# Attention on one Trainium2 core: where the softmax sums divide, the probabilities or two blocks' outputs

## The chip, the cores and the metric

The kernel runs on one core of one Trainium2 chip. The metric is the device time of one execution in microseconds (us). Three executions of the kernel before took 1732.94, 1730.12 and 1730.2 us, a median of 1730.2. The engines are called as in the profile: PE (matrix products; PEld is its weight load), DVE (vector), ACT (activation functions), POOL, and SP, which only issues DMAs; SPq, PEldq and the like are the engines' sequencers.

## What is computed

Two layers of a hybrid backbone over 512 latent tokens and 256 context tokens, width 1024. The change touches layer 0, windowed attention with a learned sink per head, 16 query heads and 4 key/value heads:

```python
def block(b):
    ...
    s_ctx = jnp.einsum('bqkgd,bnkd->bkgqn', qb, k_c, preferred_element_type=jnp.float32) * scale
    s_loc = jnp.einsum('bqkgd,bnkd->bkgqn', qb, kb, preferred_element_type=jnp.float32) * scale
    s_loc = jnp.where(valid, s_loc, NEG_INF)
    sink_col = jnp.broadcast_to(sink_g, s_ctx.shape[:-1] + (1,))
    p = jax.nn.softmax(jnp.concatenate([s_ctx, s_loc, sink_col], axis=-1), axis=-1).astype(vb.dtype)
    return (jnp.einsum('bkgqn,bnkd->bqkgd', p[..., :L], v_c)
            + jnp.einsum('bkgqn,bnkd->bqkgd', p[..., L:L + band], vb))
```

The output projection `o_x @ w_o` follows, and the same attention for the context queries over the context keys alone. Layer 1 (retention) and both feed-forward parts are untouched.

## The kernel before, in words

**Tiling.** Attention goes over four groups `g` of four query heads that share a key/value head, and in each group over six blocks of 128 queries: four latent ones, `(0, b)`, and two context ones, `(1, b)`. A block has 512, 640 or 256 keys. The order of the blocks is latent then context in groups 0 and 1, `mixed` in group 2, `late` in group 3 (L832 to L840). After blocks 1 and 3 of groups 0 to 2 the next heads' queries are made by `make_q` (L559), whose long projections on PE (L147 to L149) are the work that fills PE between the blocks' short products.

**One block.** `score` (L685) runs per head: PE multiplies queries by keys into one of three PSUM banks (L710), DVE adds the mask and takes the running extreme (L711), and per pair of heads ACT takes the exponential with the row sum (`lnexp`, shown at L101), DVE the reciprocals of the two sums (L721). Then the probabilities are divided: the second head of the pair on ACT (L725), the first on DVE (L727). `turn` (L731) transposes the four heads' probabilities per 128 keys on PE (L736) and copies them out of PSUM, in turn on ACT and on DVE (L738). `output` (L743) multiplies them by the values on PE (L750): `O` has a head's 64 features on a half of the partitions (heads 0 and 1 of the group on the lower half, 2 and 3 on the upper), and the queries along the row. In groups 0 to 2 DVE copies `O` to `o_raw`, one tile of 512 columns for a pair of blocks (L765). `splits_o` (L776) cuts `o_raw` later, during groups 2 and 3, into the high and low parts that the output projection multiplies; `parts_o` (L835) is the order of these pieces and `PARTS_AT` how many go behind each block.

**What sets the order.** The instructions are written block by block; a scheduler orders each engine's instructions by its own estimate, within the dependencies. `after(x, others)` adds an order to it: `x` stands behind `others`, with no wait on a semaphore of its own. Each engine works its list in order, and so does SP with its DMAs: in this part the next queries' halves (L605), weights (L122), and towards the end the residual streams (L181, L174). Tiles come from rings: `sq` has two buffers, shared by the squares of `make_q` (written by ACT at L585, read by PE at L617) and by later users; `res` has twelve, `stat` four, `pr` (probabilities) nine, `tt` (transposed) eight.

Of the kernel before, what the change touches and what calls it, by code (L numbers as in the profile page):

```python
# [8 lines left out]
F32 = mybir.dt.float32  # L9
# [5 lines left out]
P = 128  # L15
D = 1024
KT = D // P
SX = 512
# [3 lines left out]
NKV = 4  # L22
# [27 lines left out]
def dit_kernel(ctx, tc, xT, cT, crow, small, consts, masks, tabs0, tabs1, jtab, adaQ, adaN, adaT, wst, out):  # L50
    nc = tc.nc
# [10 lines left out]
    def T(pool, cols, tag, bufs, dt=F32):  # L62
        return pool.tile([P, cols], dt, tag=tag, bufs=bufs, name=tag)
# [27 lines left out]
    def after(ins, others):  # L91
        for o in others:
            tc.add_manual_dep(ins.ins, o.ins.name, order, reason="table set turn")
# [69 lines left out]
    def split(t, hi, lo, behind=()):  # L163
        after(nc.scalar.copy(hi, t), behind)  # L164
        return nc.vector.tensor_tensor(lo, t, hi, op=sub)  # L165
# [19 lines left out]
    def t_sq(n):  # L185
        return T(rp, 512, "sq", 2)[:, :n]
# [186 lines left out]
    raw = []  # L373
# [294 lines left out]
    psA2 = At.enter_context(tc.tile_pool(name="psA2", bufs=1, reuse_waits="tile", space=PSUM))  # L668
    pS = lambda: T(psA2, 512, "S2", 3)

    run_dep = mybir.DependencyInfo(mybir.DependencyClass.Sync, mybir.DependencyReason.DATA)
    o_raw = {}
    o_t = [[None] * KT, [None] * KT]

    class Block:
# [9 lines left out]
        def score(self, i):  # L685
            g, s, b, n = self.g, self.s, self.b, len(self.keys) * P
            hd, nl = 4 * g + i, len(self.lk) * P
            if i % 2 == 0:
                self.st = T(ap, 16, "stat", 4)
            st, c = self.st, 2 * (b + 4 * s)  # L690
            qt = q[hd, s][:, b * P:(b + 1) * P]
            pt = T(ap, 656, "pr", PRB)[:, :n + 1]
            top = stats[hd][:, 1, c + hd % 2:c + hd % 2 + 1]
            nc.gpsimd.tensor_copy(pt[:, n:n + 1], top)
            lo, x0 = st[:, i % 2:i % 2 + 1], self.lk[0] * P if nl else 0

            if nl == 384:
                runs = [(nl, SC, 5 * P, [(0, SC, kc)]), (0, nl, 2 * P, [(0, nl, kx)])]
            elif nl == 0:
                runs = [(0, SC, 5 * P, [(0, SC, kc)])]  # L700
            elif b == 0:
                runs = [(0, n, 3 * P, [(0, nl, kx), (nl, SC, kc)])]
            else:
                runs = [(0, n, 0, [(0, SC, kc), (SC, nl, kx)])]
            for c0, w, m0, parts in runs:
                bank = pS()[:, :w]
                for p0, pw, kk in parts:
                    for r in range(2):
                        keys = kk[g][r] if kk is kc else kk[g][r][:, x0:x0 + pw]
                        nc.tensor.matmul(bank[:, p0:p0 + pw], qt, keys, start=r == 0, stop=r == 1)  # L710
                nc.vector.tensor_tensor_reduce(pt[:, c0:c0 + w], bank, mask[:, m0:m0 + w], 1.0, top, add, ALU.min, lo)  # L711
                top = lo
            self.pr.append(pt)
            if i % 2 == 0:
                return
            y = stats[hd][:, 0, c:c + 2]
            nc.vector.scalar_tensor_tensor(st[:, 2:4], st[:, 0:2], -1.0, y, mult, mult)  # L717
            for e in range(2):
                pt = self.pr[i - 1 + e]
                lnexp(pt, pt, AF.Exp, scale=y[:, e:e + 1], bias=st[:, 2 + e:3 + e], accum_out=st[:, 4 + e:5 + e])  # L720
            nc.vector.reciprocal(st[:, 6:8], st[:, 4:6])  # L721
            for e in range(2):
                pt = self.pr[i - 1 + e]
                if e:
                    nc.scalar.activation(pt[:, :n], pt[:, :n], AF.Identity, scale=st[:, 6 + e:7 + e])  # L725
                else:
                    nc.vector.tensor_scalar(pt[:, :n], pt[:, :n], st[:, 6 + e:7 + e], None, op0=mult)  # L727
            if i == 3:
                self.tt = []
# [13 lines left out]
        def output(self):  # L743
            g, s, b = self.g, self.s, self.b
            O = pO()[:, :256]
            for ki, (t, tt) in enumerate(zip(self.keys, self.tt)):
                vg = vt[t][:, g * HD:(g + 1) * HD]
                f, l = ki == 0, ki == len(self.keys) - 1
                for e in range(2):
                    ins = nc.tensor.matmul(O[64 * e:64 * e + 64, :], vg, tt[:, 256 * e:256 * e + 256], start=f, stop=l)  # L750
                    if f:
                        tc.add_manual_dep(ins.ins, self.last.ins.name, run_dep, reason="value products in one run")
            if g == NKV - 1:
                if b == 0:
                    for e in range(2):
                        o_t[s][2 * g + e] = h_tiles(s)
                for e in range(2):
                    hi, lo = o_t[s][2 * g + e]
                    cs = slice(b * P, b * P + P)
                    split(O[:, e * P:e * P + P], hi[:, cs], lo[:, cs])  # L760
                return
            if b % 2 == 0:
                o_raw[g, s, b // 2] = T(rp, 512, "res", 12)
            dst = o_raw[g, s, b // 2].rearrange("p (e b q) -> p e b q", e=2, b=2)[:, :, b % 2, :]
            nc.vector.tensor_copy(dst, O.rearrange("p (e q) -> p e q", e=2))  # L765

    def attend(g, s, b):
        blk = Block(g, s, b)
        for i in range(4):
            blk.score(i)  # L770
        for ki in range(len(blk.keys)):
            blk.turn(ki)
        blk.output()
        return blk.copy

    def splits_o(g, s, bp):  # L776

# [47 lines left out]
    def context_out(d, w):  # L825
# [6 lines left out]
    latent, context = [(0, b) for b in range(4)], [(1, b) for b in range(2)]  # L832
    mixed = [latent[0], latent[1], context[0], latent[2], latent[3], context[1]]
    late = [context[0], latent[0], context[1], latent[1], latent[2], latent[3]]
    parts_o = [p for sb in ((0, 0, 0), (0, 1, 0), (1, 1, 0), (2, 1, 0), (0, 0, 1), (1, 0, 0), (1, 0, 1),  # L835
                            (2, 0, 0), (2, 0, 1)) for p in splits_o(*sb)]
    PARTS_AT = {(2, 4): 2, (2, 5): 3, (3, 0): 3, (3, 1): 2, (3, 2): 2, (3, 3): 2, (3, 4): 2, (3, 5): 2}
    for g in range(NKV):
        final = g == NKV - 1
        for i, (s, b) in enumerate((latent + context, latent + context, mixed, late)[g]):  # L840
            copy = attend(g, s, b)
            if not final and i in (1, 3):
                for piece in make_q(2 * g + 2 + i // 3):
                    piece()
            if (g, i) >= SPLIT_AT:
                first = len(parts_o) == 18
                for _ in range(PARTS_AT[g, i]):
                    parts_o.pop(0)([copy])
                if first:
                    wo0 = wpos[0]  # L850
                    cres = load_stream(1)
            for d in {3: early[:1], 4: early[1:3], 5: early[3:]}.get(i, ()) if final else ():
                wpos[0] = wo0 + d
                wo_w[d] = next_w(ap, 0)
                context_out(d, wo_w[d])
# [1102 lines left out]
```

## Time and profile before

| what | us |
|---|---|
| median of three executions | 1730.2 |
| the profiled execution | 1731.61 |
| its span | 1729.8 |
| attention (first scores to last output product) | from 99 to 314 of the span |
| PE busy, whole span | 1700.0 (98%) |
| DVE busy, whole span | 1361.1 (79%) |
| ACT busy, whole span | 870.4 (50%) |

A busy PE is not a PE at its full rate: its products are pipelined, a product of 256 columns is shown with 0.28 us and follows the one before after 0.12. So the chain of waits, which follows the end back through what released each step, says more on the bound than the busy share. All durations in the prediction are of the profiled execution.

### The profile page before, as it was taken

How to read it: one execution, taken by the hardware profiler on the slowest of the kernel's cores; microseconds unless marked ns; L12 is line 12 of the kernel's file. 1: busy time of each engine (PE TensorE's matmuls, PEld its weight loads, DVE VectorE, ACT ScalarE, POOL GpSimd, SP SyncE). 2: the span in 40 equal slices, each digit the busy share in tenths (PEclk: the TensorE clock that was granted, in tenths of full speed). 3: DMA queues.
4: the chain of work that ended last, by engine and by line, in shares of the span. 5: the costliest groups of instructions: out<-in, count | busy, mean ns of one | idle time of the engine just before them, and what ended most of it. 6: DMA issues, size and time to landing. Idle time of an engine off the chain costs nothing.

```text
span 1729.8 us, 27790 instructions
## 1 busy us (share of the span) xinstructions
PE 1700.0 (98%) x10876; PEld 1515.2 (88%) x10876; DVE 1361.1 (79%) x2436; ACT 870.4 (50%) x1552; POOL 50.4 (3%) x168
## 2 busy tenths in 40 slices
PE   7999999999999999999999999999999999999999
PEld 5788877899999999999988788898897899999988
DVE  6698889798778788787889858858758798877774
ACT  5587779565434334342556534524525565445442
POOL 0000000000000000000000000000000000000000
PEclk9999999999999999999999999999999999999999
DMA  9612221643244434453423524524423223333322
GB/s 356 232 30 57 62 62 56 209 133 123 74 150 121 156 110 149 122 155 102 156 99 88 182 76 134 161 83 125 157 89 108 91 81 106 115 109 111 98 86 86
DMA packets 62803, 207.48 MB, mean 120 GB/s; under 512 B 7248, under 2 KB 8912, under 8 KB 62416
## 3 DMA queue, kind: packets, MB, share of 16 engines
q1 hardware_dynamic: 55184, 178.97, 32.5%
q0 software_dynamic: 7200, 26.22, 5.1%
q8 instruction: 85, 1.39, 0.3%
q10 hardware_dynamic: 288, 0.52, 0.1%
q14 instruction: 46, 0.38, 0.1%
HBM read 199.65 MB, written 2.10 MB: 117 GB/s over the span
## 4 chain that ended last, share of the span: by engine, by line
PE 79%; DVE 12%; DMA 5%; ACT 2%; issue 2%; SPq 0%; DVEq 0%; ACTq 0%
PE Y L897 15%; PE Z L897 8%; PE pj L147 7%; PE pj L149 7%; PE pj L148 7%; PE X L897 4%; DMA wraw<-in_wst_dram 4%; PE Z L1292 4%; DVE wlo L165 3%; PE pT L736 2%; PE pO L750 2%; PE S L710 2%; PE X L149 1%; PE X L147 1%; PE X L148 1%
## 5 line engine op out<-in xcount | busy, mean ns | idle before, releaser
L164 ACT CAST whi<-wraw 128x1024 fp32r<-128x1024 f32 x258 | 270.0, 1051 | 335.9 <-PE Z L149 80.1
L165 DVE TENSOR_TENSOR wlo<-wraw,whi 128x1024 fp32r<-128x1024 f32 x258 | 314.2, 1221 | 64.8 <-ACT whi L164 62.9
L897 PE MATMUL Y<-aq,whi 128*128 128x384 f32 x640 | 173.7, 335 | 0.0
L897 PEld LDWEIGHTS Y<-aq,whi 128*128 128x128 f32 x640 | 116.6, 188 | 1.1 <-ACT hn L1053 1.1
L256 DVE SCALAR_TENSOR_TENSOR res<-pj,mod,res 128x512 f32<-128x512 f32 (+1 forms) x112 | 81.0, 728 | 39.4 <-PE pj L149 39.2
L273 DVE CUSTOM_DVE_ANT_0 y<-adaw,crow,small_sb 128x1024 bf16<-128x1024 f32 x64 | 81.9, 1280 | 32.2 <-DMA adaw<-in_adaT_dram 32.0
L897 PE MATMUL Y<-aq,wlo 128*128 128x384 f32 x320 | 107.0, 334 | 0.0
L1292 PE MATMUL Z<-whi,sA 128*128 128x512 f32 x256 | 81.5, 393 | 1.3 <-ACT gate L1479 1.2
L101 ACT ACTIVATE pr<-pr,stat,qs 128x513 f32<-128x513 f32 (+2 forms) x96 | 74.2, 775 | 9.1 <-DVE stat L717 8.8
L147 PE MATMUL pj<-ax,whi 128*128 128x512 f32 x176 | 69.1, 393 | 0.4 <-DVE res L256 0.4
L149 PE MATMUL pj<-ax,whi 128*128 128x512 f32 x176 | 68.7, 390 | 0.0
L148 PE MATMUL pj<-ax,wlo 128*128 128x512 f32 x176 | 68.6, 390 | 0.0
L147 PE MATMUL pj<-act,whi 128*128 128x512 f32 x168 | 65.6, 390 | 0.0
L148 PE MATMUL pj<-act,wlo 128*128 128x512 f32 x168 | 65.5, 390 | 0.0
L149 PE MATMUL pj<-act,whi 128*128 128x512 f32 x168 | 65.5, 391 | 0.0
L897 PEld LDWEIGHTS Y<-aq,wlo 128*128 128x128 f32 x320 | 60.1, 188 | 0.0
L711 DVE CUSTOM_DVE_ANT_0 pr<-S,mask,qs 128x256 f32<-128x256 f32 (+1 forms) x96 | 53.1, 566 | 7.9 <-PE S L710 5.4
L1292 PEld LDWEIGHTS Z<-whi,sA 128*128 128x128 f32 x256 | 48.0, 188 | 12.6 <-ACT gate L1479 2.1
L897 PE MATMUL Y<-sA,whi 128*128 128x256 f32 x304 | 58.1, 277 | 0.1
L897 PE MATMUL Y<-hx,whi 128*128 128x256 f32 x304 | 56.3, 277 | 0.0
L736 PE MATMUL pT<-const_sb,pr 128*128 128x128 f32 x352 | 54.1, 280 | 1.2 <-ACT tt L738 0.9
L736 PEld LDWEIGHTS pT<-const_sb,pr 128*128 128x128 f32 x352 | 40.2, 142 | 12.0 <-issue 4.0
(581 smaller groups left out, 5085.4 us busy)
## 6 DMA issues: line engine op xcount, KB each, us to landing
wraw<-in_wst_dram SPq DMA_DIRECT2D x224, 512.0 KB, 3.7
adaw<-in_adaT_dram POOLq DMA_DIRECT2D x48, 512.0 KB, 3.9
wx<-in_wst_dram SPq DMA_DIRECT2D x30, 512.0 KB, 4.3
adan<-in_adaQ_dram SPq DMA_DIRECT2D x16, 512.0 KB, 8.7
adan<-in_adaN_dram SPq DMA_DIRECT2D x12, 512.0 KB, 8.1
adaw<-in_adaT_dram SPq DMA_DIRECT2D x8, 512.0 KB, 3.9
res<-in_xT_dram SPq DMA_DIRECT2D x14, 256.0 KB, 2.8
aq<-in_adaN_dram SPq DMA_DIRECT2D x12, 256.0 KB, 5.7
```

Source lines behind the costliest of these rows:

```text
L101: ins = nc.scalar.activation(*args, **kw)
L147: nc.tensor.matmul(o, whi, xhi, start=first, stop=False)
L148: nc.tensor.matmul(o, wlo, xhi, start=False, stop=False)
L149: return nc.tensor.matmul(o, whi, xlo, start=False, stop=last)
L164: after(nc.scalar.copy(hi, t), behind)
L165: return nc.vector.tensor_tensor(lo, t, hi, op=sub)
L256: return nc.vector.scalar_tensor_tensor(res[d], o, mods[l, s][:, part, d:d + 1], res[d], mult, add)
L273: res.append(nc.vector.tensor_tensor_reduce(junk, w, cr[:, s * 1024:(s + 1) * 1024], 1.0, sm_t[:, C_ADAB + l * 48 + j:C_ADAB + l * 48 + j ...
L711: nc.vector.tensor_tensor_reduce(pt[:, c0:c0 + w], bank, mask[:, m0:m0 + w], 1.0, top, add, ALU.min, lo)
L736: nc.tensor.transpose(tp[:, a * P:(a + 1) * P], self.pr[(0, 2, 1, 3)[a]][:, ki * P:(ki + 1) * P], ident)
L897: nc.tensor.matmul(o, p, r, start=first and k + i == 0, stop=k == 3 and i == 2, skip_group_check=not first)
L1292: ins = nc.tensor.matmul(os[t], p, r, start=first and k + i == 0, stop=k == 3 and i == 2, skip_group_check=by_k or not first)
```

## The change

In groups 0 to 2 the probabilities are no longer divided. The two reciprocals of each pair of heads are written by a DMA to a tile in DRAM, as rows over the queries. Two blocks after a pair of blocks is complete, two DMAs read the pair's rows back, each spread over 64 partitions, and one DVE instruction multiplies the `o_raw` tile of both blocks by them. Group 3 divides as before. The ring `stat` grows from 4 to 12 buffers, and the pieces of `(2, 1, 0)` move two places back in `parts_o`.

```diff
@@ -668,6 +668,8 @@
+    rows = At.enter_context(tc.tile_pool(name="rows", bufs=1, reuse_waits="tile", space=bass.MemoryType.DRAM))
+    factor_rows, row_end, o_end = {}, [None], [None]
@@ -686,7 +688,7 @@
             if i % 2 == 0:
-                self.st = T(ap, 16, "stat", 4)
+                self.st = T(ap, 16, "stat", 12)
@@ -719,6 +721,14 @@
             nc.vector.reciprocal(st[:, 6:8], st[:, 4:6])
+            if g < NKV - 1:
+                if i == 1 and b % 2 == 0:
+                    factor_rows[g, s, b // 2] = rows.tile([2, 2, 2, P], F32, tag="row", bufs=9, name="row")
+                row = factor_rows[g, s, b // 2][:, i // 2, b % 2, :]
+                row_end[0] = nc.sync.dma_start(row.rearrange("e q -> q e"), st[:, 6:8])
+                if i == 3:
+                    self.tt = []
+                return
             for e in range(2):
@@ -757,12 +767,12 @@
-                    split(O[:, e * P:e * P + P], hi[:, cs], lo[:, cs])
+                    o_end[0] = split(O[:, e * P:e * P + P], hi[:, cs], lo[:, cs])
                 return
...
-            nc.vector.tensor_copy(dst, O.rearrange("p (e q) -> p e q", e=2))
+            o_end[0] = nc.vector.tensor_copy(dst, O.rearrange("p (e q) -> p e q", e=2))
@@ -772,6 +782,13 @@
+    def scale_o(g, s, bp):
+        raw, factor = o_raw[g, s, bp], t_sq(SX)
+        row = factor_rows[g, s, bp].rearrange("e j b q -> e (j b q)")
+        for e in range(2):
+            after(nc.sync.dma_start(factor[64 * e:64 * e + 64, :], row[e:e + 1, :].broadcast_to([64, 512])), row_end)
+        after(nc.vector.tensor_tensor(raw, raw, factor, op=mult), o_end)
@@ -832,13 +849,18 @@
-    parts_o = [p for sb in ((0, 0, 0), (0, 1, 0), (1, 1, 0), (2, 1, 0), (0, 0, 1), (1, 0, 0), (1, 0, 1),
+    parts_o = [p for sb in ((0, 0, 0), (0, 1, 0), (1, 1, 0), (0, 0, 1), (1, 0, 0), (2, 1, 0), (1, 0, 1),
                             (2, 0, 0), (2, 0, 1)) for p in splits_o(*sb)]
+    unscaled = []
     for g in range(NKV):
...
             copy = attend(g, s, b)
+            while unscaled and unscaled[0][0] + 2 <= 6 * g + i:
+                scale_o(*unscaled.pop(0)[1])
+            if not final and b % 2:
+                unscaled.append((6 * g + i, (g, s, b // 2)))
```

Lines of the changed kernel are later by 2 to 22: L711 becomes L713, L721 L723, L727 L737, L736 L746, L738 L748, L750 L760, L765 L775. New are L728 (the write of the rows), L790 (the two reads) and L791 (the multiplication). There are 36 writes, 18 reads and 9 multiplications.

The scheduler sets many instructions elsewhere. Three places follow; `ISA` in these lists is L711's (now L713's) instruction, in two parts.

First DVE in group 0, where the first block's second pair has its reciprocals and the second block's scores come in. Before:

```order
L721 RECIPROCAL stat<-stat 128x2
L717 SCALAR_TENSOR_TENSOR stat<-stat,qs 128x2
L711 ISA pr,stat<-S_1441,mask,stat 128x384
L711 ISA stat 128x1
L727 TENSOR_SCALAR pr<-pr,stat 128x512
L711 ISA pr,stat<-S_1447,mask,qs 128x256
L711 ISA stat 128x1
L589 STREAM_SHUFFLE y_1544<-hn 128x512
L738 COPY tt<-pT 128x512
L711 ISA pr,stat<-S_1451,mask,stat 128x384
L711 ISA stat 128x1
L590 TENSOR_TENSOR hn<-hn,rope_175 128x512
```

Now:

```order
L723 RECIPROCAL stat<-stat 128x2
L713 ISA pr,stat<-S_1437,mask,qs 128x256
L713 ISA stat 128x1
L748 COPY tt<-pT 128x512
L719 SCALAR_TENSOR_TENSOR stat<-stat,qs 128x2
L713 ISA pr,stat<-S_1441,mask,stat 128x384
L713 ISA stat 128x1
L713 ISA pr,stat<-S_1447,mask,qs 128x256
L713 ISA stat 128x1
L748 COPY tt<-pT 128x512
L713 ISA pr,stat<-S_1451,mask,stat 128x384
L713 ISA stat 128x1
```

The division L727 is gone, and the two copies of transposed probabilities stand two to three places earlier among the scores.

Second SP in group 0, from block 2 to the context blocks (`q<-y` and `q<-hn` are the next queries' high and low halves, `y_1841` those that `make_q` makes behind block 3; `sq<-row` are the two reads for the first pair of blocks). Before:

```order
L122 DMA wraw<-in_wst_dram 128x1024 x2
L605 DMA q<-y_1841 64x512
L605 DMA q<-hn 64x512
L605 DMA q<-y_1841 64x512
L605 DMA q<-hn 64x512
L605 DMA q<-y_1879 64x256 x2
L605 DMA q<-hn 64x256 x2
```

Now:

```order
L728 DMA row<-stat 128x2x1 x2
L122 DMA wraw<-in_wst_dram 128x1024
L728 DMA row<-stat 128x2x1 x2
L790 DMA sq<-row 64x512 x2
L605 DMA q<-y_1841 64x512 x2
L605 DMA q<-hn 64x512 x2
L605 DMA q<-y_1879 64x256 x2
L728 DMA row<-stat 128x2x1
L605 DMA q<-hn 64x256 x2
```

The weights' load and the queries' halves stand behind writes that need a reciprocal, and the halves behind the two reads as well.

Third DVE at the end of the fourth block of group 2 (latent block 2 in the `mixed` order), where the last `make_q` runs out. Before:

```order
L592 TENSOR_TENSOR hn<-hn,y_3203 128x512
L738 COPY tt<-pT 128x512
L711 ISA pr,stat<-S_3266,mask,qs 128x512
L711 ISA stat 128x1
L609 TENSOR_TENSOR q<-hn,q 64x512
L165 TENSOR_TENSOR wlo<-wraw,whi 128x1024
L765 COPY res<-pO 128x2x128
L199 SCALAR_TENSOR_TENSOR qs<-pj,qs 128x12
L610 TENSOR_TENSOR q<-hn,q 64x512
L609 TENSOR_TENSOR q<-hn,q 64x256
L610 TENSOR_TENSOR q<-hn,q 64x256
L200 SCALAR_TENSOR_TENSOR qs<-qs 128x12
```

Now:

```order
L592 TENSOR_TENSOR hn<-hn,y_3210 128x512
L775 COPY res<-pO 128x2x128
L791 TENSOR_TENSOR res<-res,sq 128x512
L713 ISA pr,stat<-S_3273,mask,qs 128x512
L713 ISA stat 128x1
L609 TENSOR_TENSOR q<-hn,q 64x512
L610 TENSOR_TENSOR q<-hn,q 64x512
L609 TENSOR_TENSOR q<-hn,q 64x256
L610 TENSOR_TENSOR q<-hn,q 64x256
L713 ISA pr,stat<-S_3281,mask,qs 128x512
L713 ISA stat 128x1
L199 SCALAR_TENSOR_TENSOR qs<-pj,qs 128x12
```

The multiplication stands directly behind the copy of the block's output and ahead of the next block's first scores; the split of a weight tile (L165) and L199 have moved behind the second scores.

## The prediction

> **What bounds the kernel now.** I read the page's chain of waits first, then the busy time by stage, then the chain inside the attention.
>
> ```profile
> PE 79%; DVE 12%; DMA 5%; ACT 2%; issue 2%; SPq 0%; DVEq 0%; ACTq 0%
> ```
>
> ```profile
> core 0: us, PE busy (x) PEld busy (x) DVE busy (x) ACT busy (x) POOL busy (x), PEclk, DMA share, GB/s
> ...
> 109.00:122.00 13.00, 11.91 (x83) 8.98 (x82) 12.60 (x44) 10.40 (x21) 1.01 (x4) 1.00 0.02 4
> 122.00:169.00 47.00, 46.41 (x335) 37.61 (x335) 38.78 (x131) 37.22 (x86) 4.64 (x24) 1.00 0.23 60
> 169.00:175.00 6.00, 5.77 (x49) 4.88 (x46) 5.02 (x13) 4.92 (x10) 0.00 (x0) 1.00 0.25 83
> 175.00:249.00 74.00, 73.56 (x538) 60.82 (x538) 59.05 (x195) 57.12 (x128) 5.88 (x36) 1.00 0.24 63
> 249.00:262.00 13.00, 9.53 (x52) 7.77 (x49) 10.23 (x38) 9.31 (x25) 0.00 (x0) 0.74 0.15 43
> ...
> 268.00:292.00 24.00, 23.08 (x168) 18.42 (x165) 22.10 (x88) 21.27 (x55) 1.72 (x12) 1.00 0.18 55
> ```
>
> PE bounds the kernel, and the change takes no product from it. Of the three changed groups (to about 268) PE is full for 121 us (122 to 169, 175 to 249: 46.41 of 47.00 and 73.56 of 74.00), and there work taken from DVE and ACT is worth nothing. It can only be worth something in two stretches: 109 to 122, where DVE is full (12.60 of 13.00), and 249 to 262, where nobody is, PE waits, and its clock falls (0.74). The chain inside those two, and the instructions in time around the second:
>
> ```profile
> 113.43 0.40 DVE pr L727
> ...
> 118.02 0.47 DVE pr L727
> ...
> 120.41 1.08 PE S L710 x4
> ```
>
> ```profile
> by line: DVE pr L711 31.2%; PE pT L736 17.4%; DVE q L610 11.2%; ACT pr L101 9.9%; issue 7.5%; ACT tt L738 5.9%; DVE pr L727 5.7%; DVE q L609 4.2%; DVE stat L717 3.1%; DVE stat L721 2.5%; DVE qs L200 1.7%; DVE stat L711 1.3%; DVE qs L624 1.1
> 251.72 0.69 DVE q L610
> ...
> 253.51 0.66 DVE pr L711
> ...
> 259.05 0.50 DVE pr L727
> ...
> 259.68 1.19 PE pT L736 x5
> ...
> 261.53 0.55 PE pT L736 x3
> ```
>
> ```profile
> 174.81 0.44 PE pT L736 x4
> ...
> 246.04 0.79 PE pj L617 x8
> ```
>
> ```profile
> 240.72 0.17 DVE L721 RECIPROCAL stat<-stat 128x2 f32<-128x2 f32 x1 [1.13 <-ACT pr L101]
> ...
> 250.45 0.42 DVE L765 COPY res<-pO 128x256 f32<-128x256 f32 x1
> ...
> 254.33 3.45 PE L710 MATMUL S<-kc,q 128*128 128x256 f32 x10 [2.54 <-DVE qs L620]
> ...
> 256.50 0.72 ACT L725 ACTIVATE pr<-pr,stat 128x512 f32<-128x512 f32 x1 [0.32 <-DVE stat L721]
> ...
> 257.12 0.81 ACT L101 ACTIVATE pr<-pr,stat,qs 128x513 f32<-128x513 f32 x1
> ```
>
> The division is a small part of these chains: 5.7% of the ten microseconds behind 252.
>
> **What is removed.** Twelve divisions of each width on ACT and on DVE, 72 of the 96:
>
> ```profile
> L725 ACT ACTIVATE pr<-pr,stat 128x640 f32<-128x640 f32 x12 | 9.9, 828 | 2.3 <-DVE stat L721 2.3
> L725 ACT ACTIVATE pr<-pr,stat 128x512 f32<-128x512 f32 x12 | 8.5, 719 | 1.5 <-DVE stat L721 1.5
> L725 ACT ACTIVATE pr<-pr,stat 128x256 f32<-128x256 f32 x13 | 6.5, 503 | 1.5 <-DVE stat L717 0.8 <-DVE stat L721 0.7
> ```
>
> ```profile
> L727 DVE TENSOR_SCALAR pr<-pr,stat 128x640 f32<-128x640 f32 x12 | 6.6, 549 | 0.1
> L727 DVE TENSOR_SCALAR pr<-pr,stat 128x512 f32<-128x512 f32 x12 | 5.8, 482 | 0.2
> L727 DVE TENSOR_SCALAR pr<-pr,stat 128x256 f32<-128x256 f32 x13 | 4.5, 347 | 0.0
> ...
> L592 DVE TENSOR_TENSOR hn<-hn,y 128x512 f32<-128x512 f32 x6 | 4.1, 681 | 0.0
> ```
>
> ACT loses 12 x (0.828 + 0.719 + 0.503) = 24.6 us, DVE 12 x (0.549 + 0.482 + 0.347) = 16.5. **Added on DVE**: nine multiplications of 128x512, each like L592, 0.68, so 6.1 in all, net -10.4. By the full stretches nearly all of that lies under PE. What is on the path:
>
> (a) 109 to 122. Three divisions stand on DVE ahead of the scores that release PE at 120.41; 0.40, 0.47 and one before of the first's width, 0.40, make -1.3. It is 0 if DVE's freed places go to other work. PE idles 1.09 of these 13 us (13.00 - 11.91) and could close up its pipelined products by about as much again: -2.2 at most.
>
> (b) 169 to 175 lies between the two full stretches, with 0.23 us of idle PE: -0.3, from 0 to -1.
>
> (c) 249 to 262. PE stands 2.54 us for a bank that the scores on DVE must free. From the copy of `O` at 250.45 to that release it is 3.9. The new list has, from the copy on, the copy (0.42), a multiplication (0.68), the first scores (0.66), four halves of queries (two of 0.69, two of half the width at about 0.42) and the second scores (0.66): 4.6, or 4.4 with the overlaps that the starts show. But it gives PE eight more L617 products and a head's four score products behind the end of `O`, 0.79 on the chain and some 0.5 more, 1.3 us of cover: 3.9 + 1.3 - 4.4 = 0.8 less. Behind it ACT's exponential at 257.12 starts as the division at 256.50 ends, 0.6 late; the division at 259.05 holds the transposes for 0.50, the hop through the reciprocal 0.2. The transposes then run at a lowered clock:
>
> ```profile
> 254.00:258.00 4.00, 3.50 (x13) 2.90 (x13) 4.00 (x21) 3.21 (x8) 0.00 (x0) 0.50 0.02 6
> 258.00:262.00 4.00, 3.24 (x17) 2.75 (x17) 2.29 (x10) 3.71 (x12) 0.00 (x0) 0.68 0.01 2
> ```
>
> Eight of them take 1.74 us on the chain (1.19 and 0.55), against some 0.9 at the full clock (0.44 for four at 174.81); I take all of that 0.8, since nowhere else in these stretches is the clock below 1.00 and the stall that goes before it gets a third shorter. Sum of (c): -0.8 - 0.6 - 0.5 - 0.2 - 0.8 = -2.9; from +0.7 (the multiplication alone is paid) to -5 (no stall of 2.5, no lowered clock at 0.8, the 1.3 behind it, and 0.4 for the scores at half clock). The Trainium skill (TensorE: Matmul & The Clock Gate, part 1) says the clock halves after an idle window of about 3.4 us, free-running; the 0.50 behind a stall of 2.54 agrees in kind, and by that rule whether it falls hangs on the phase, so the 0.8 would be all or nothing, and the sum -2.9 or -2.1.
>
> (d) 262 to 268, the last block's divisions, 128x256: one of them on the path, as ACT's 0.50: -0.5, from 0 to two, -1.
>
> (e) 268 to 292, group 3, keeps its divisions and is near DVE's bound (22.10 of 24.00). Two of the nine multiplications land in it, 1.4 at L592's duration; since DVE is full for nine tenths of it but PE too, I take half: +0.7, from 0 to +1.4.
>
> **The new DMAs.** No row shows a write of four-byte pieces. Issue and landing are bounded by:
>
> ```profile
> L605 SPq DMA_DIRECT2D q<-y x20: 461/537/597, 120.6 to 233.1; - x20
> ...
> DMA to landing us min/median/max: 1.9/2.3/4.4
> ```
>
> ```profile
> q1 hardware_dynamic: 55184, 178.97, 32.5%
> ...
> out_dram<-res SPq DMA_DIRECT2D x8, 256.0 KB, 2.0
> ```
>
> A write has 256 pieces, the half of a query tile 64. If SP's issue does not depend on the pieces it is 0.54, if it does 4 x 0.6 = 2.4; I take 0.54, since whole and half rows issue within 0.46 to 0.60 alike. Landing: 2.0 as the stores of the output, up to 2.0 + 16 pieces per DMA engine at the mean packet's 0.163 us (32.5% of 16 x 1729.8 us over 55184) = 4.6; the reads come two blocks later, so either is covered. SP then has 54 more issues, 29 us (29 to 97) in 150, so it is not a bound. Behind its waits stand the query halves and the weights; PE waits for those. For the halves:
>
> ```profile
> 198.76 0.59 SPq L605 DMA_DIRECT2D q<-hn  x1
> ...
> 209.49 0.16 DVE L721 RECIPROCAL stat<-stat 128x2 f32<-128x2 f32 x1
> ...
> 214.54 0.42 DVE L765 COPY res<-pO 128x256 f32<-128x256 f32 x1
> ```
>
> The halves issued at 198.76 are for heads whose scores come behind that context block, ten microseconds later; two reads (1.1) and a write (0.5) ahead of them are hidden. If that cover were gone each would cost PE its 1.6.
>
> **The added wait.** The multiplication waits on DVE for its row. From the block's last reciprocal to the copy of its output passed 9.7 us (240.72 to 250.45), 5.0 in a context block (209.49 to 214.54), and a division less now. The row needs 0.5 (last write, ahead of the reads in SP's list) + 1.1 + 2.3 = 3.9, so it has landed; behind the context blocks' copies the new list puts one to three microseconds of other work first. Cost 0; with the upper bounds 2.4 + 1.2 + 4.4 = 8.0 it is at the edge. Behind a waiting multiplication stand the next block's scores, and on ACT the squares of the next queries, which take over its `sq` buffer.
>
> **Sum:** -1.3 - 0.3 - 2.9 - 0.5 + 0.7 = -4.3 on a span of 1729.8, 1725.5. That execution took 1731.61, 1.4 over the median of 1730.2; on the median it is 1730.2 - 4.3 = 1725.9. All parts at their ends give -9.2 and +2.1, 1721 to 1732.
>
> **Rivals.**
>
> *Given back* (0.12): PE's list is as long as before, and what DVE and ACT finish sooner stands in front of the same banks; only (a) counts and (e) eats it: -1.3 + 0.7, so 1729.6. For it: 121 us of full PE. Against: both stretches have divisions on the chain.
>
> *The hole closes* (0.22): DVE and ACT, 10 and 25 us lighter, are far enough ahead at 249 that PE never stands there; (c) at -5, (a) at -2.2, (b) and (d) at -1: -9.2, 1721.
>
> *The row is late* (0.24): the write's pieces cost SP and the DMA engines in proportion. From about 9 us behind the reciprocal it decides, since the copy came at 9.7 and a division less is now ahead of it: at 11 the five multiplications behind latent blocks each hold DVE 2 us, and by the `sq` ring ACT too, +10, less 4.3: 1735.9. For it: no such row exists. Against: 8.0 by the upper bounds. By the Trainium skill (DMA: Bandwidth & Descriptors, rules for kernel authors) a non-contiguous last dimension becomes one descriptor per element, to be avoided; that speaks for this rival, and no run here shows its price. By its section Specifications, transfers under 512 B are read and modified too.
>
> **Chances.** The forecast has 0.42. Less than 0.2% (3.5 us) this kernel's measurement can't tell from no change, and 1725.9 lies 0.8 past that. Faster: two thirds of the forecast's case (0.28) and the closed hole, 0.50. Same: the rest of the forecast's (0.14) and nearly all that is given back, 0.25. Slower: the late row and a little, 0.25. The range reaches down past the closed hole and up into the late row: 1719 to 1735; the forecast's own is 1721.5 to 1730.
>
> **What would show it.** Right: in 109 to 122 PE has its scores about a microsecond sooner; between 249 and 262 the wait of 2.54 is under 2; the nine multiplications wait for no DMA; PE full in the two long stretches; the end of attention 4 us earlier and all behind it shifted by as much. Wrong: a DVE or ACT wait on the reads, queries' halves late at a group's start, a new hole of PE in 122 to 249, or a hole at the turn to group 3 as long as before.

## The result, and the profile after

| | us |
|---|---|
| before, median of 5 runs | 1730.2 (1730.12 to 1732.94) |
| after, median of 5 runs | 1786.04 (1784.3 to 1788.84) |
| ratio | 1.0318, 95% interval 1.0303 to 1.0333 |
| predicted | 1725.9, 1719 to 1735 |
| span of the profiled execution after | 1784.2 |
| end of the attention (end of the last output product) | 314.3 before, 367.1 after |

The kernel became 3.2% slower. The attention ends 52.9 us later, and from there to the end of the span it is 1415.6 us before and 1417.0 after: the loss lies in the attention. The page of the profile after shows the chain of waits, by engine and by line:

```profile
PE 72%; DMA 11%; DVE 11%; ACT 3%; issue 2%; SPq 0%; DVEq 0%; ACTq 0%
PE Y L919 14%; PE Z L919 7%; PE pj L149 6%; PE pj L147 6%; PE pj L148 6%; DMA sq<-row 4%; PE Z L1314 4%; PE X L919 3%; DMA wraw<-in_wst_dram 3%; DVE wlo L165 3%; PE S L712 2%; PE X L149 1%; PE X L147 1%; PE X L148 1%; PE pT L746 1%
```

PE has lost 7 of its 79%, DMA gained 6, and a new entry stands among the lines: `DMA sq<-row`, the reads of the rows, with 4% of the span. The list of waits inside the attention (who waited for whom: us in total, times, longest) says whom they hold:

```profile
...
DVE res L791 <- DMA sq<-row: 38.9, 8, 10.4
PEld S L712 <- DVE stat L713: 28.7, 13, 9.5
PE S L712 <- DVE stat L713: 24.4, 8, 9.2
...
ACT y L164 <- DMA q<-y: 8.8, 2, 7.5
```

Eight of the nine multiplications waited, 38.9 us together, and PE's waits for a score bank are what that makes of it. The last row is another matter: ACT waited for query halves, a DMA that was there before. The chain of waits around the first multiplication (start, duration, what) shows the first path, the rows of DVE at the same place what stood there:

```profile
144.30 0.36 SPq L728
...
144.75 0.48 SPq L790
...
145.28 14.20 DMA sq<-row
...
159.57 0.06 DVE res L791
...
160.86 0.40 DVE pr L713
...
161.32 0.80 PE S L712 x2
```

```profile
152.37 0.42 DVE L775 COPY res<-pO 128x256 f32<-128x256 f32 x1
159.57 0.69 DVE L791 TENSOR_TENSOR res<-res,sq 128x512 f32<-128x512 f32 x1 [6.78 <-DMA sq<-row]
```

The pair's last row is written at 144.30, the reads are issued 0.45 us behind it, and the second needs 14.20 us to land. DVE, done with the copy at 152.8, stands for 6.78 us in front of the multiplication, with the next scores behind it; PE gets its first bank 1.8 us after that. The second path, before there is any multiplication, in SP's timeline and in the chain:

```profile
119.33 0.36 SPq L728 DMA_DIRECT2D row<-stat  x1
119.78 0.54 SPq L605 DMA_DIRECT2D q<-y  x1
...
120.37 0.58 SPq L605 DMA_DIRECT2D q<-y  x1
```

```profile
120.37 10.49 DMA q<-y
...
131.25 1.02 ACT pr L101 x2
...
132.31 0.69 PE pT L746 x2
```

A query half issued 1.04 us behind a row write lands after 10.49 us; in the profile before these took 2.3. ACT's exponentials stand behind it, and PE's transposes behind those. Busy time in four stretches of the execution after shows the holes and the clock (columns as in the prediction's first stretches):

```profile
126.00:132.00 6.00, 0.23 (x2) 0.00 (x0) 0.50 (x2) 1.06 (x2) 0.00 (x0) 0.90 0.01 4
155.00:162.00 7.00, 0.94 (x6) 0.74 (x5) 2.43 (x9) 0.75 (x2) 0.00 (x0) 0.72 0.14 21
180.00:187.00 7.00, 0.68 (x4) 0.63 (x4) 2.57 (x8) 0.00 (x0) 0.14 (x2) 0.64 0.62 28
...
290.00:299.00 9.00, 0.03 (x1) 0.00 (x0) 1.14 (x2) 2.55 (x7) 0.00 (x0) 0.76 0.73 122
```

PE is all but idle in each, and behind each it runs at half its clock for a while. From 97 us to the end of the attention PE's gaps sum to 7.1 us before and 44.1 after, and the clock is at 0.50 for 6.8 us before and 54.6 after: 37 us of the 52.9 are standstill; the other 16 fit the lowered clock, as far as it fell on work.

The times from a DMA's issue on SP to the last of its landing signals, counted in each trace from 97 us to the end of the attention, show which DMAs are slow (median, longest in brackets; the columns on the right are experiments 1, 3, 5 and 7 below):

| us | before | after | two pieces | writes only | far pieces | transposed |
|---|---|---|---|---|---|---|
| row writes | | 9.7 (16.5) | 1.1 (4.2) | 8.9 (16.2) | 1.7 (4.2) | 1.2 (2.7) |
| row reads | | 9.8 (16.3) | 2.9 (4.0) | | 2.9 (3.1) | 3.0 (3.5) |
| `q<-y` halves | 2.3 (3.6) | 3.0 (10.9) | 2.2 (3.7) | 3.8 (10.0) | 2.2 (3.3) | 2.2 (4.1) |
| weights, L122 | 3.7 (5.2) | 6.5 (17.9) | 3.5 (5.5) | 6.4 (12.2) | 3.7 (5.2) | 3.5 (4.6) |

Most of the query halves and weights are issued when no row write is on its way, so their medians move less than their longest times. In the execution after, a query half issued 0.5 us behind the latest row write landed after 10.9, one issued 5.9 behind after 5.7, and one 10.0 behind after 1.7.

### The profile page after: what moved, and what is told of

Its sections match the earlier page's. It is cut to its first block, busy times and chain, and to the rows that moved or that the text cites. A ratio compares the mean times of both kernels' runs of the same rounds, so it can differ in the third digit from the quotient of the medians.

```text
span 1784.2 us, 27807 instructions
## 1 busy us (share of the span) xinstructions
PE 1716.0 (96%) x10876; PEld 1525.1 (85%) x10876; DVE 1354.7 (76%) x2409; ACT 851.4 (48%) x1516; POOL 50.9 (3%) x168
## 3 DMA queue, kind: packets, MB, share of 16 engines
q1 hardware_dynamic: 66416, 181.37, 34.3%
## 4 chain that ended last, share of the span: by engine, by line
PE 72%; DMA 11%; DVE 11%; ACT 3%; issue 2%; SPq 0%; DVEq 0%; ACTq 0%
PE Y L919 14%; PE Z L919 7%; PE pj L149 6%; PE pj L147 6%; PE pj L148 6%; DMA sq<-row 4%; PE Z L1314 4%; PE X L919 3%; DMA wraw<-in_wst_dram 3%; DVE wlo L165 3%; PE S L712 2%; PE X L149 1%; PE X L147 1%; PE X L148 1%; PE pT L746 1%
## 5 line engine op out<-in xcount | busy, mean ns | idle before, releaser
L165 DVE TENSOR_TENSOR wlo<-wraw,whi 128x1024 fp32r<-128x1024 f32 x258 | 314.3, 1221 | 64.8 <-ACT whi L164 62.7
L746 PE MATMUL pT<-const_sb,pr 128*128 128x128 f32 x352 | 58.6, 291 | 12.6 <-ACT pr L101 6.1
L712 PE MATMUL S<-kc,q 128*128 128x256 f32 x192 | 46.0, 334 | 24.9 <-DVE stat L713 22.9
L746 PEld LDWEIGHTS pT<-const_sb,pr 128*128 128x128 f32 x352 | 42.1, 147 | 25.5 <-ACT pr L101 7.9
L712 PEld LDWEIGHTS S<-kc,q 128*128 128x128 f32 x192 | 35.2, 221 | 29.5 <-DVE stat L713 25.3
```

What stands on the lines that cost most here:

```text
L746: nc.tensor.transpose(tp[:, a * P:(a + 1) * P], self.pr[(0, 2, 1, 3)[a]][:, ki * P:(ki + 1) * P], ident)
```

## The experiments

Theory A: a row write of 256 four-byte pieces needs some 10 us to land, and every DMA issued behind it lands after it, the reads and DMAs that have nothing to do with it. Rivals: B, the broadcast reads are slow; C, the new order on DVE, ACT and PE makes the holes; D, the multiplications just stand too early. Ratios are to the kernel before, run on the same chip beside each kernel; its medians there were 1731.9 to 1732.5.

### 1. The same kernel with two pieces to a write

```diff
-                row_end[0] = nc.sync.dma_start(row.rearrange("e q -> q e"), st[:, 6:8])
+                row_end[0] = nc.sync.dma_start(row, cst[0:2, 0:P])   # and a wait for the reciprocals
```

> The changed kernel with its instructions in the same order on every engine; each of the 36 row writes moves the same 1 KB to the same place at the same point of SP's list, still behind its reciprocals, but as 2 pieces of 512 bytes instead of 256 of 4 bytes (it copies two rows of the constant matrix, so the reciprocals themselves are left out and the outputs are scaled by ones and zeros). Theory A (a write of 256 four-byte pieces takes some 9 to 10 us and whatever is issued behind it on the queue lands behind it): the writes land in 2 to 3 us, the reads in about 2.5, no multiplication waits for its row, and the time falls by all of the 53 us lost in the attention and the 4 of the forecast, 1722 to 1732. Rival B (the broadcast reads are slow, 64 partitions on one 2 KB row): the reads still land 9 us or more behind their issue, 1765 to 1786. Rival C (the new order on DVE, ACT and PE makes the holes): 1770 or more with the DMAs quick.

Measured: 1732.68, ratio 1.0004 (0.9994 to 1.0013). The order of instructions is that of the changed kernel, and 53.4 us are gone; B and C fall. The two rows of the multiplications (group, then busy time, mean ns, idle before and for whom), of the changed kernel and of this one:

```profile
L791 DVE TENSOR_TENSOR res<-res,sq 128x512 f32<-128x512 f32 x9 | 6.2, 690 | 38.9 <-DMA sq<-row 38.9
```

```profile
L791 DVE TENSOR_TENSOR res<-res,sq 128x512 f32<-128x512 f32 x9 | 6.1, 681 | 0.0
```

The last column falls from 38.9 to nothing. But the 4.3 us of the forecast are not in the median either. In the profiled execution the attention ends at 312.6, 1.6 earlier than before. Three of its stretches:

```profile
109.00:122.00 13.00, 12.39 (x98) 10.48 (x96) 12.27 (x41) 10.04 (x22) 0.89 (x7) 1.00 0.09 21
...
247.00:262.00 15.00, 11.72 (x80) 9.76 (x78) 13.36 (x48) 12.18 (x31) 0.79 (x4) 0.89 0.07 24
...
268.00:292.00 24.00, 21.95 (x157) 17.25 (x156) 21.88 (x82) 20.95 (x53) 1.53 (x11) 1.00 0.19 63
```

PE's idle time is 13.00 - 12.39 = 0.61 in the first (1.09 before), 15.00 - 11.72 = 3.28 in the second (3.47 before), and there the clock costs 15 x 0.11 = 1.7 instead of 13 x 0.26 = 3.4; in the third it is 2.05, up from 0.92.

### 2. No rows and no multiplications

The writes, the reads and the multiplications are taken out; the outputs of the three groups stay unscaled.

> The changed kernel without writes, reads and the nine multiplications: outputs of the first three groups stay unscaled. Theory A: what is left is the removal of the 72 divisions, the forecast's gain without its cost on DVE, 1721 to 1726. Theory B: the same. Rival C: over 1735. Rival D (the divisions were hidden under PE anyway): 1728 to 1731.

Measured: 1730.19, ratio 0.9986 (0.9977 to 0.9995), and the attention ends at 312.5. This is what the removal of 72 divisions is worth by itself: 0.14%, some 2 us (0.9 to 4.0 by the interval), inside rival D's 1728 to 1731 and not the 5.0 that terms (a) to (d) had for it. C falls once more. The third stretch of this kernel:

```profile
268.00:292.00 24.00, 23.05 (x164) 18.20 (x162) 21.42 (x83) 21.48 (x53) 1.53 (x11) 1.00 0.14 45
```

PE's idle time there is 0.95, as before; with rows and multiplications it was 2.05.

### 3. The writes alone

```diff
-            after(nc.sync.dma_start(factor[64 * e:64 * e + 64, :], row[e:e + 1, :].broadcast_to([64, 512])), row_end)
-        after(nc.vector.tensor_tensor(raw, raw, factor, op=mult), o_end)
+        after(nc.vector.tensor_tensor(raw, raw, rope0[:, 0:512], op=mult), o_end)
```

> The changed kernel with its 36 writes of 256 pieces, but nothing is read back: the nine multiplications take a factor that lies in the chip's memory already (the cosine table), so the outputs are scaled wrongly. Theory A: the multiplications wait for no DMA, which takes 38.9 us of waiting away, but the query halves and the weights issued behind a write still land 10 us late: 1733 to 1752, with waits of ACT or PE for query halves and weights. Rival B: all of the loss is gone, 1722 to 1730.

Measured: 1746.02, ratio 1.0091 (1.0067 to 1.0114). Nobody reads the rows, and the writes alone cost 1746.02 - 1732.68 = 13.3 us. The wait that the list shows for it:

```profile
ACT y L164 <- DMA q<-y: 13.4, 4, 6.7
```

So the 53.4 us split into about 40 that go with the waiting multiplications and about 13 that other DMAs lose behind the writes. The split is rough: the four executions lie between 1743.52 and 1751.72, and without the reads the scheduler has set some of the instructions of DVE and PE elsewhere.

### 4. What a write costs by itself

The kernel before, with single DMAs behind its last store, each issued when the one ahead has landed. They write columns of the constant matrix to tiles in DRAM that nobody reads.

> The kernel before with a chain of single DMAs behind its last store, each issued when the one ahead has landed: writes to memory of 256, 128, 512 and 64 pieces of 4 bytes, 128 of 8, 256 of 4 bytes each into a line of its own, 128 of 64 bytes, 128 of 512, 2 of 512; the broadcast read; a 512 KB load alone, behind a write of 256 pieces on the same queue, and behind one on ACT's queue. Theory A1 (time by the number of pieces, some 17 on each DMA engine at about 0.5 us): 256 pieces land in 8 to 10 us, 512 in 16 to 19, 128 in 5, 64 in 3, far ones as long as near ones, and 128 of 64 bytes in 5. Theory A2 (pieces in one line of memory stand in each other's way): far ones and those of 64 bytes land in 2 to 4 us, 256 near ones in 9. Under both the load behind a write lands 6 us or more later than alone. Rival B: the write lands in 2 to 5 us and the broadcast read in 8 or more.

Measured, in the list of DMA issues (KB, us from issue to landing). `w256x` is the write of the change, `w128x` with 0.5 KB one row of it, `w512x` four rows, `w64x` 64 such pieces, `far` has its pieces 512 bytes apart, `w128x` with 1 KB is 128 pieces of 8 bytes and with 8 KB 128 of 64 bytes, both without gaps, `r64x` the broadcast read:

```profile
load<-in_wst_dram SPq DMA_DIRECT2D x1, 512.0 KB, 3.6
loadA<-in_wst_dram SPq DMA_DIRECT2D x1, 512.0 KB, 11.9
loadB<-in_wst_dram SPq DMA_DIRECT2D x1, 512.0 KB, 10.1
...
r64x<-in_masks_dram SPq DMA_DIRECT2D x1, 128.0 KB, 2.9
...
w256x<-const_sb SPq DMA_DIRECT2D x2, 1.0 KB, 7.8
w128x<-const_sb SPq DMA_DIRECT2D x1, 0.5 KB, 7.4
w512x<-const_sb SPq DMA_DIRECT2D x1, 2.0 KB, 10.4
w64x<-const_sb SPq DMA_DIRECT2D x1, 0.2 KB, 6.0
w128x<-const_sb SPq DMA_DIRECT2D x1, 1.0 KB, 3.2
w256x4far<-const_sb SPq DMA_DIRECT2D x1, 1.0 KB, 1.5
w128x<-const_sb SPq DMA_DIRECT2D x1, 8.0 KB, 1.4
```

A1, time by the number of pieces, falls: half the pieces take 7.4 instead of 7.8, a quarter 6.0, twice as many 10.4, and as many with room between them 1.5. What is slow is many small pieces side by side; experiment 8 says how small. The read alone lands in 2.9, which ends B. A load of 512 KB, 3.6 alone, needs 11.9 behind a write (`loadA`), and 10.1 when ACT's queue issued the write at the same moment (`loadB`): another queue is no way out. The Trainium skill (DMA: Bandwidth & Descriptors, Queues, rings and completion order) says that the two queues share the same 16 engines and that a DMA's landing signal comes only after every earlier write of its engine, across queues; the 10.1 agrees.

### 5. As many pieces, 64 bytes apart

```diff
-                    factor_rows[g, s, b // 2] = rows.tile([2, 2, 2, P], F32, tag="row", bufs=9, name="row")
-                row = factor_rows[g, s, b // 2][:, i // 2, b % 2, :]
+                    factor_rows[g, s, b // 2] = rows.tile([2, 2, 2, P, 16], F32, tag="row", bufs=9, name="row")
+                row = factor_rows[g, s, b // 2][:, i // 2, b % 2, :, 0]
```

> The changed kernel with as many pieces of 4 bytes in each of its 36 row writes, but each piece 64 bytes from the next; the reads, still behind their writes and at their places, fetch two rows of a table, so the outputs are scaled by that table and not by the reciprocals. Theory A2 (pieces within one short stretch of memory wait for each other): the writes land in 1.5 to 2.5 us as with 2 pieces, and the time is that of the two-piece kernel, 1730 to 1735. Theory A1 (the number of pieces sets the landing): writes of 8 to 10 us and 1770 to 1790 as with near pieces.

Measured: 1732.0, ratio 0.9997 (0.9988 to 1.0006). In its list of DMA issues:

```profile
sq<-in_tabs_dram SPq DMA_DIRECT2D x18, 128.0 KB, 2.9
...
row<-stat SPq DMA_DIRECT2D x36, 1.0 KB, 1.7
```

The 256 pieces remain, and at nearly the same place in SP's list (the scheduler moved a few instructions) they cost nothing that can be measured when they lie apart.

### 6. The multiplication one block later

```diff
-                scale_o(*unscaled.pop(0)[1])
+                n, pair = unscaled.pop(0)
+                read.append((n, scale_o(*pair)))
+            while read and read[0][0] + 3 <= 6 * g + i:
+                multiply(*read.pop(0)[1])
```

> The changed kernel with each multiplication one block later (three behind its pair instead of two) while its two reads stay at their place; the order in which two parts of the third group are split moves with it. Theory A: the reads still land about 10 us behind their issue, but a block lasts about 8 us, so the 38.9 us of waiting by the multiplications fall to under 12; the late query halves and weights stay, so the time is that of the writes alone or a little over, 1744 to 1758. Rival D (the multiplications stand too early and nothing else is wrong): 1730 to 1736. Rival E (the factor now holds a buffer of the ring of the queries' squares a block longer): ACT waits for that ring and the time is 1760 or more.

Measured: 1752.36, ratio 1.0119 (1.0104 to 1.0133). In the list of waits the rows for a DMA are

```profile
ACT y L164 <- DMA q<-y: 10.4, 4, 6.8
...
DVE hn L165 <- DMA q<-hn: 1.6, 1, 1.6
...
DVE res L794 <- DMA sq<-row: 0.3, 1, 0.3
```

L794 is the multiplication here: one of the nine still waits, 0.3 us where it was 38.9 in all. D falls in part: a block of distance recovers some 34 of the 53 us. The rest, 20, stays; the writes still hold the query halves, and the attention ends at 328.0, near the 325.7 of the writes alone, but the rest of the span is 4.6 longer than before, which stays open (experiment 9 comes back to it). E is next to nothing: ACT's squares wait once for a multiplication to give the ring's buffer free, 0.5 us.

### 7. The rows by way of a transposition

VectorE turns squares of 32 (128x32 in 0.21 us here), so a pair's rows leave as 32 pieces of 128 bytes:

```diff
+                nc.vector.reciprocal(rt[:, 0:8].rearrange("p (e x) -> p e x", e=2)[:, :, i // 2 * 2 + b % 2], st[:, 4:6])
+                if i == 3 and b % 2:
+                    nc.vector.transpose(rT, rt)
+                    row_end[:] = [nc.sync.dma_start(row[:, 32 * c:32 * c + 32], rT[32 * c:32 * c + 8, :]) for c in range(4)]
```

> The changed kernel, whole, with another way to its rows: the reciprocals of two blocks lie in 8 columns of one tile, VectorE transposes that in squares of 32 (9 more DVE instructions), and a pair's rows are written by 4 DMAs of 8 pieces of 128 bytes instead of 4 of 256 pieces of 4. Theory A: the writes land in 1 to 2 us, no multiplication waits for its row, and the time is that of the two-piece kernel, 1730 to 1735; the interval against the kernel before holds 1. Theory A1 with a fixed cost for each write: the same. Rival C: over 1740.

Measured: 1731.88, ratio 0.9996 (0.9987 to 1.0005). In this run pairs of the third group shared a tile of reciprocals, so some of its outputs are scaled by another pair's; runs 9 and 10 have a tile for each. The change without its late rows is worth nothing that can be measured.

### 8. How close is close

> The kernel before with a second chain of single writes behind its last store, each issued when the one ahead has landed: 256 pieces of 4 bytes every 8, 16, 32, 64, 128 and 256 bytes; a row of 128 pieces of 4 bytes in order and with neighbours 64 bytes apart in time (the same places in another order); 128 pieces of 16 and of 32 bytes without gaps; 8 of 128 bytes; a 512 KB load behind a write of 256 near pieces on the same queue and on ACT's. Theory A2 with a unit of 64 bytes: the landing falls in proportion to the pieces in a unit, about 8 us with 16, 4 to 5 with 8, 3 with 4, 2 with 2 and 1.5 from 64 bytes on; 128 pieces of 16 bytes in 2 to 3. With a unit of 512 bytes: 256 bytes apart is still slower than 1.5, and 64 apart lands in 4 us or more. The order within a row makes no difference if pieces queue at the memory; if the conflict is between pieces that come one behind the other it lands in under 3 us.

Measured, us from issue to landing:

```profile
every8B<-const_sb SPq DMA_DIRECT2D x1, 1.0 KB, 2.9
every16B<-const_sb SPq DMA_DIRECT2D x1, 1.0 KB, 1.6
...
every64B<-const_sb SPq DMA_DIRECT2D x1, 1.0 KB, 1.7
...
row<-const_sb SPq DMA_DIRECT2D x1, 0.5 KB, 7.5
rowmixed<-const_sb SPq DMA_DIRECT2D x1, 0.5 KB, 6.8
w128x16B<-const_sb SPq DMA_DIRECT2D x1, 2.0 KB, 1.4
w128x32B<-const_sb SPq DMA_DIRECT2D x1, 4.0 KB, 2.1
```

Neighbours, 4 bytes apart, take 7.5 a row; one gap of 4 bytes brings 256 of them to 2.9, a step of 16 bytes to 1.6, and more room adds nothing. That falls faster than in proportion and fits neither unit of A2 as it was put. Pieces of 16 bytes without any gap between them (`w128x16B`) land in 1.4, so touching is not what costs either. What the slow writes share is more than one piece in 16 bytes: with two (a step of 8 bytes, or the 8-byte pieces of experiment 4) 2.9 and 3.2, with four 6.0 to 10.4. That is a pattern in single probes; why it is so was not shown. The same places in another order take 6.8: it is where pieces lie, not which come one behind the other. The load behind such a write was late again, 12.4 on the same queue and 10.5 on the other.

### 9. The multiplications on GpSimd

> The changed kernel, whole: its rows by the transposition in squares of 32 and writes of 128-byte pieces, and the nine multiplications on GpSimd instead of VectorE. Theory F (with quick rows, what is left of the change's cost is the nine multiplications on DVE in the third group's end and the fourth group): the time is that without rows and multiplications, 0.9986 of the kernel before, 1728 to 1731, and the PE idle time of 268 to 292, 2.05 us with two pieces, is about 1 again. Rival G (a multiplication on GpSimd is slow or holds up VectorE, with which it reads the same memory): DVE's scores take longer meanwhile, or the splits wait for GpSimd, 1732 to 1738.

Measured: 1732.31, ratio 1.0003 (0.9994 to 1.0012). GpSimd takes 1.38 us each, twice DVE's:

```profile
L801 POOL TENSOR_TENSOR res<-res,sq 128x512 f32<-128x512 f32 x9 | 12.4, 1379 | 7.9 <-DMA sq<-row 7.9
```

F falls: off DVE, they bring nothing in the time, though PE's idle time in 268 to 292 goes from 2.05 to 1.37. The time is in rival G's range, but DVE's scores take as long as before (0.478 us for 256 keys). The attention ends at 312.6, within 0.3 of runs 1, 2 and 5. What eats the gain comes behind it: from there to the end of the span it is 1415.6 before, 1416.0 without rows and 1415.7 with the writes alone, but 1419.2, 1418.5, 1420.2, 1419.8 and 1420.2 in runs 1, 5, 6, 7 and 9, and 1417.0 in the changed kernel itself. Each is a single execution, and those of 1, 5, 7 and 9 were 0.9 to 2.7 us longer than their medians, so part of it is scatter. In these four PE waits 1.75 to 2.25 us for one weight tile at about 1329 (0.86 before, 0.58 without rows), and in three of the four its clock then halves for 3.41 us. But with the writes alone PE waits 2.21 for the same tile, and its stretch is no longer than before: the wait is not the whole of it. Every kernel with the 18 reads is longer there (run 10 too, 1417.2) and none without them, and run 9 has the same lists behind the attention as the kernel before; the cause stays open.

### 10 and 11. One more edit at the hole

At 250 a hole was left in every version: 2.54 us before, 2.30 or 2.31 in runs 1, 2, 5 and 9, 3.04 in run 7. There DVE and ACT make the halves of the eighth query unit.

```diff
-            if 1 < j < 7:
+            if 1 < j < 8:
```

> The changed kernel, whole, with rows by the transposition as above and the multiplications on DVE, and the halves of the eighth query unit moved by 8 DMAs like those of units 2 to 6, where both kernels so far make them by four copies on ACT and four subtractions on DVE. These stand in front of the scores on DVE at the one hole of PE that is left in the attention (2.3 us and a halved clock, at 250). Theory H (the hole is DVE's work there): DVE is 2.2 us shorter at that place, the hole and its halved clock go, 1727 to 1730. Rival I (the halves land 2 to 3 us behind their subtraction and that is as late as DVE was): the hole stays and the time is 1731 to 1735.

> The kernel before with that one edit, the halves of the eighth query unit by 8 DMAs. Theory H: its hole of 2.54 us and its lowered clock go, 3 to 5 us less, 1727 to 1730. Rival I: 1731 to 1736. It also tells what of the run above is the change and what is this edit.

Measured: with the change and quick rows 1726.69, ratio 0.9974 (0.9965 to 0.9983), attention ending at 309.4; the kernel before with that edit 1731.3, 0.9998 (0.9989 to 1.0006). The edit alone gains nothing in the median, nor the change alone (run 7, 0.9996), both together 5.2 us, and that version beats both kernels. In the profiled executions the attention ends at 314.3 before, 312.8 with the change alone, 313.1 with the edit alone and 309.4 with both, which is more than the two gains added. Theory H came true with the change, a little below its range, and not without it: there the hole of 2.54 goes, but the time stays in rival I's range. PE's longest wait in the stretch, first of the kernel before with the edit, then of the changed one with it:

```profile
257.86 1.46 PE L736 MATMUL pT<-const_sb,pr 128*128 128x128 f32 x6 [0.99 <-ACT pr L725]
```

```profile
250.69 0.47 PE L715 MATMUL S<-kc,q 128*128 128x256 f32 x2 [0.77 <-DVE qs L200]
```

With the query halves out of the way the next thing that PE waits for in the kernel before is a division on ACT, L725, and its clock halves for 3.41 us right behind. The changed kernel has no such division and its clock stays at 1.00. The division had been behind another wait of the same hole: neither edit shows in the time without the other.

## Why the prediction was wrong, step by step

**The added wait: the step that failed.** "Cost 0" rested on a row that has landed 3.9 us after the last reciprocal: 0.5 + 1.1 + 2.3. Measured from the issue of the last write (144.30) to the landing of the second read (159.48) it is 15.2, and the median write takes 9.7. The upper bound of 4.6 shared the pieces out over 16 DMA engines at the mean packet's time; the packets do go out fast (those under 64 bytes took 0.009 us in the median of the attention after), but their landing does not follow from them (experiment 4: 256 pieces in 7.8 or in 1.5). The bound came from rows of large transfers, and none of those writes neighbours in small pieces. The prediction said itself that no row shows such a write, and then bounded it too tightly. Three of its own signs of being wrong showed: DVE waits on the reads, query halves come late, and PE has new holes at 126, 155 and 180.

**The new DMAs on SP.** SP's issue, taken at 0.54 from bounds 0.54 and 2.4, was well chosen: 0.36 us. The halves behind them, "hidden", were not: the cover was counted against 1.6 us of issue time, and it was the landing, 10.49 us, that had to be hidden. What these halves and the weights lose is the 13 us of experiment 3.

**The rival *The row is late*** named the place and the mechanism, with a chance of 0.24, and its chain is the one seen: late row, DVE, scores, PE. Its price was 10 us and is 53. It let five multiplications wait 2 us, where eight waited 38.9 in all; it left out the lowered clock behind every hole, and the DMAs that queue behind the writes. Its reason, cost in proportion to the pieces, is wrong too. Of the Trainium skill's rule against it (DMA: Bandwidth & Descriptors, rules for kernel authors), one descriptor per element holds: the queue's packets grew by 66416 - 55184 = 11232, which is 36 x 272 + 18 x 80: 256 pieces and 16 landing signals for a write, 64 and 16 for a read. But the count does not set the price (experiment 5).

**The gain, with the late rows taken away** (PE's idle time and clock loss of experiment 1 against before): (a) forecast -1.3, measured 0.61 - 1.09 = -0.5 in idle time. But busy PE gave more: the rows show 98 products in 109 to 122 instead of 83, and 15 products, each 0.12 behind the one ahead, are 1.8 us by an estimate; the first output product starts at 115.7 instead of 117.3. The prediction had named this closing up and counted it only in its bound of -2.2, so (a) was not too large. The long full stretch, forecast -0.3 under (b), gave 0.41 - 1.26 = -0.8. (c) forecast -2.9: the clock gave 1.7 where 0.8 was taken, the waits 0.2 where 2.1 were; the hole stayed (2.30 of 2.54), since the query halves stand in it whatever the divisions do. (d) forecast -0.5, measured -0.4. (e) forecast +0.7, measured +1.1 in 268 to 292, and nothing without the rows and multiplications (experiment 2). Idle time and clock together make -2.5 up to 292; at the end of the attention -1.6 is left instead of -4.3, and in the medians it cannot be told from none. The term that failed here is the wait in (c): parts of a chain were counted as gained though another wait of the same hole, the query halves, stood beside them. How much of what (a) gave was lost again in the full stretches the idle times do not tell.

***Given back*** (0.12), 1729.6 by its own sum and 0.6 less than before, is what the kernel with quick rows shows within the measurement, but by other amounts than its two terms. ***The hole closes*** (0.22) did not happen by the change; with the edit of experiment 10 its longest wait falls to 0.77, at 1726.7 and not the 1721 of that rival.

## What to carry to other kernels

A DMA that scatters a column into neighbouring four-byte places of DRAM is slow to land (some 10 us here) and holds what is issued behind it until then: turn it on the chip first, so that it leaves in longer pieces, and price a new DMA by what lands behind it, not by its issue. Where a transfer's like is not in the profile, one probe of it alone is worth more than a bound from other shapes. A stretch can give back PE's idle time, its clock loss and what its products can close up, so count all three; and a hole with two causes gives next to nothing until both are gone.

## What the runs showed of the hardware that was not expected

Writing 256 neighbouring 4-byte pieces to DRAM lands in 7.8 us alone and in 8.8 and 9.2 with a load issued just behind, with a step of 8 bytes in 2.9, of 16 or more in 1.5 to 1.8, and 2 pieces of 512 bytes about as fast (1.1 in the kernel). By the Trainium skill (DMA: Bandwidth & Descriptors, Specifications) transfers under 512 bytes are read and modified too; the runs show that being under 512 bytes is not what costs here (128 pieces of 16 bytes without a gap land in 1.4), having several pieces within 16 bytes is. Whether pieces wait for each other in the memory was not shown, nor was such a write into on-chip memory tried.

PE's clock was lowered for 3.41, 6.83, 10.24 or 13.65 us, whole multiples of 3.41, and already behind single waits of 0.99 us (experiment 11, after several shorter ones) and 2.3 us, while waits of 1.99 (run 7, at 1329) and 2.21 us (run 3, at 1341) left it at 1.00. So the length of one wait does not tell whether the clock falls.
